# A decoder layer on one core: the input projection in K groups of 2, 2, 4, 4, 4 in place of 4, 4, 4, 4

## The chip, the core and the metric

The kernel runs on one core of a Trainium2 chip. The metric is the device time of one execution in microseconds, lower is better. The core has TensorE (matmuls, weights loaded beside them), VectorE, ScalarE and GpSimd, and SyncE, whose queue here issues every DMA, in order. All are named in the profile as PE (weight loads PEld), DVE, ACT, POOL and SP. Each engine works through its instructions in a fixed order.

## What is computed

One layer over 256 tokens of width 2048, in float32: four token mixers on one shared input projection, an output projection, and a gated feed-forward part, each behind an RMSNorm whose result is scaled and shifted by six modulations that come from a conditioning vector c.

```python
cond = silu(c)
mod = (cond @ w_mod + b_mod).reshape(B, 6, D)          # w_mod: 2048 x 12288
sh1, sc1, g1, sh2, sc2, g2 = [mod[:, i, None, :] for i in range(6)]
h = rmsnorm(x, norm_mix) * (1.0 + sc1) + sh1
proj = h @ w_in                                        # w_in: 2048 x 5660
y = mixers(proj)                                       # GLA, gated DeltaNet, pooling, forgetting attention
x = x + g1 * (y @ w_out)
h = rmsnorm(x, norm_ffn) * (1.0 + sc2) + sh2
x = x + g2 * conv_ffn(h, ...)
out = rmsnorm(x, norm_final)
```

What matters here: no column of the projection can be finished before all 2048 rows of `h` are known, and a row of `h` is known only when its two modulations are summed over all 2048 rows of `w_mod`. A K tile is 128 of those rows of `h`, so there are 16.

## The kernel before

**Precision.** Every weight is loaded as float32 and split into a rounded high part (ScalarE, line 115) and a low part (VectorE, line 100, called from `split`). A product is three matmuls: high by high, high by low, low by high. A load is always [128, 1024] words, 512 KB: four K tiles of 256 columns, or two of 512 (`load_split`, lines 153 to 163; five buffers for loads, three for the parts).

**The groups.** The K tiles are worked through in groups, `GROUPS` (line 46), before 4, 4, 4, 4. For a group three things are needed:

- `mods(g)` (335 to 365) loads w_mod, one DMA for each of the 16 row tiles and always for the columns of this group's shift and scale, 512 KB for four K tiles, and accumulates each on VectorE into one tile `ga` (line 361, the operation at 103 or 107). When the sixteenth is in, TensorE sums `ga` over its partitions (line 345, two instructions for each of 2 x 4 matmuls), VectorE adds the biases (346 to 349), and `h` of the group's K tiles is formed and split into `HL` (`bigA` in the profile). There are five buffers for the loads, `wm`, and one `ga`.
- `gdn(g)` (410 to 424) multiplies the group's K tiles with the 1536 columns of DeltaNet's queries, keys and values. Its sums stay in six PSUM banks (`acc`) over all groups.
- `extras(g)` (470 to 474) visits pairs of column tiles among the other 4096 columns, 16 pairs in all (the comment at line 48 speaks of 18). A visit (`pair`, 438 to 459) loads 256 columns of all K tiles that this pair has not yet had, multiplies them into one of two PSUM banks (`ext`), and adds the bank to the pair's place in SBUF: the first visit by a copy on ScalarE (line 430), the later ones by an addition on VectorE (435, 437, the operation at 100 or 103).

`TAKE` (line 49) says how many of the 16 pairs each group but the last visits, counted from the last pair: 16, 12, 11. In the last group all pairs are visited, with whatever K tiles they still lack; that is 25 loads of 512 KB. These visits are not made beside `gdn` but among the mixers, as filler for TensorE: `gated_deltanet()` is issued first, and the loop at 921 interleaves the visits with the mixers. With each load of a visit, `paced` (908) also takes 0.38 and 0.69 of a step of two background series, the products of c with w_mod for the second half's modulations and the first gate, `bg` (506); what is left of them follows after the mixers.

**The order.** The main loop (lines 510 to 527) interleaves `mods(g + 1)` with `gdn(g)` and `extras(g)`, one w_mod load for each load of weights:

```python
for g in range(NG):
    nxt = mods(g + 1) if g < NG - 1 else iter(())
    with tc.issue_after(hold[0].ins):
        if g == NG - 1:
            small()
            gates()
        for i, _ in enumerate(gdn(g)):
            next(nxt, None)
            if g == 0 and i == 2:
                rest()
                small_load()
```

`issue_after` holds the group's weight loads behind the last w_mod load of the group's own modulations. Within these bounds a scheduler orders each engine's instructions when the kernel is built, by a model of the times; on the chip that order is fixed.

`rest()` (367 to 393) loads thirteen small vectors and constant arrays that the convolution, the mixers and the second half use, and prepares masks from them. `small_load()` (396 to 400) loads 28 narrow columns of w_in with three DMAs of short rows; `small()` (402) multiplies them in the last group, and `gates()` (257) follows.

Of the kernel before, what the change touches and what calls it, by code (L numbers as in the profile page):

```python
# [19 lines left out]
T = 256  # L20
# [8 lines left out]
# columns of w_in  # L29
# [3 lines left out]
# columns of the constant array  # L33
# [11 lines left out]
# the groups of K tiles in which w_in is worked through: first tile, how many  # L45
GROUPS = ((0, 4), (4, 4), (8, 4), (12, 4))
NG = len(GROUPS)
# how many of the 18 pairs of columns beside DeltaNet's queries, keys and values each group but the last visits
TAKE = (16, 12, 11)
# the order of the mixers: gla, pooling, forgetting attention, DeltaNet  # L50
ORDER = "gpfd"
# modulations (s: scale 2, h: shift 2, g: gate 1; half) summed on the tensor engine and on VectorE, steps per load of columns
# [4 lines left out]
def _consts():  # L57
    i = np.arange(P)
    s, t = i[:, None], i[None, :]
    same = (s // CH) == (t // CH)  # L60
    cols = [s == t, same & (s <= t), same & (s > t), s <= t, np.ones((P, P)), s > t]
    cols.append(np.where(t > s, -1e30, 0.0))
    for w in (2, 4, 8, 16):
        cols.append(np.broadcast_to(1.0 / np.minimum(np.arange(1, 17), w), (P, 16)))
    # the level at which s and t part, counted from 1 above the diagonal and from 7 below it
    lv = sum((l + 1) * ((s // (2 * m) == t // (2 * m)) & (s % (2 * m) < m) & (t % (2 * m) >= m))
             for l, m in enumerate(LEVELS))
    lw = lv.T
    cols.append(lv + np.where(lw > 0, lw + len(LEVELS), 0))
    return np.ascontiguousarray(np.concatenate([np.asarray(a, np.float32) for a in cols], axis=1))  # L70
# [3 lines left out]
def trunk_kernel(ctx: ExitStack, tc: tile.TileContext, x, c, w_mod, b_mod, norm_mix, norm_ffn, w_in,  # L74
# [53 lines left out]
    # ones in the rows 0 and 64, and in the rows 32 and 96  # L128
# [45 lines left out]
    def gemv(col0, done, pst=None, ready=lambda: True, bias=None):  # L174
        """cond * w over 1024 columns: without pst summed by partition on VectorE, else on the tensor engine,
        four column tiles side by side"""
        acc = pst() if pst else keep.tile([P, 1024], F32, name="ga", tag="ga")
        if bias is not None:
            G.memset(acc, 0.0)
            nc.sync.dma_start(acc[0:1], bias)  # L180
        for k in range(0, KT, 2):
            wms = []
            for kk in range(2):
                wms.append(wp.tile([P, 1024], F32, name="wm", tag="wm", bufs=4))
                last_wm[0] = nc.sync.dma_start(wms[kk], wm_v[:, k + kk, col0:col0 + 1024])
            for kk in range(2):
                wm = wms[kk]
                if not pst:
                    accumulate(acc, wm, k + kk, bias is None)
                    continue  # L190
                for c in range(2):
                    o = 64 * kk + 32 * c
                    mm(acc[o:o + 32], cond[:, k + kk:k + kk + 1].to_broadcast([P, 32]), wm[:, c * 512:c * 512 + 512],
                       start=k == 0, stop=k == KT - 2)
            if k == KT - 2:
                while not ready():
                    yield
                with tc.high_priority():
                    if pst:
                        gr = wp.tile([P, 1024], F32, name="wr", tag="wr", bufs=5)[:, 0:512]  # L200
                        S_.copy(gr, acc)
                        done([(gr, sel[:, c:c + 1]) for c in range(2)])
                    else:
                        done([(acc[:, c * 512:c * 512 + 512], ones) for c in range(2)])
            yield
# [21 lines left out]
    # ================= attention half =================  # L227
    with ExitStack() as ph:
# [11 lines left out]
        # projections: gla q 0:2, k 2:4, g 4:8, gdn g 8:12, pool 12:16, fox q 16:20, k 20:24  # L240
# [16 lines left out]
        def gates():  # L257
# [13 lines left out]
            # columns 0:4 1/(1+e), columns 4:12 1/(2+e)  # L271
# [16 lines left out]
        with ExitStack() as st:  # L288
# [25 lines left out]
            # 1 + b_mod of the two scales  # L314
# [19 lines left out]
            # sh1, sc1 of the K tiles of group g, then h  # L334
# [60 lines left out]
            # the small columns: lr 0:16, b 16:20, a 20:24, f 24:28; row 28 is one  # L395
# [30 lines left out]
            # one pair of column tiles over some groups of K tiles; two sums share a bank: only the first clears it  # L426
# [68 lines left out]
            # g1 takes the place of values no longer needed  # L495
# [14 lines left out]
# [3 lines that stand above are left out]
# [3 lines left out]
                    for i, _ in enumerate(gdn(g)):  # L516
                        next(nxt, None)
                        if g == 0 and i == 2:
                            rest()
                            small_load()  # L520
# [8 lines left out]
            # conv of gdn's q, k, v straight from the accumulators  # L529
# [37 lines left out]
        def gated_deltanet():  # L567
            # norms of q and k
# [12 lines left out]
            # decays within the chunk  # L581
# [17 lines left out]
            for t in range(NT):  # L599
                ts = slice(t * P, t * P + P)  # L600
                # exp of the decays, transposed: [j, i], i no earlier than j
# [8 lines left out]
                # -M^T (and its diagonal, which no level takes)  # L610
# [9 lines left out]
            # inverse of I + M by blocks of 2, 4, .. 64: X = inverse, Y = its transpose  # L620
# [30 lines left out]
            for t in range(NT):  # L651
                ts = slice(t * P, t * P + P)
                # keys and values by token
# [9 lines left out]
                # attention [j, i]  # L663
# [5 lines left out]
                # queries times the decay from the chunk's start  # L669
# [6 lines left out]
            # u and w^T, over the values' and the keys' place  # L676
# [10 lines left out]
            # the states, chunk by chunk, over M and X  # L687
# [19 lines left out]
            # outputs, normalised, in place of Y  # L707
            oss, ors = dt_("oss", zz), dt_("ors", zz)
            for t in range(NT):
# [12 lines left out]
                # r = c * (c^2 * ss / d + eps)^-1/2  # L722
# [9 lines left out]
        def finish(on_t, t, nw, i, b):  # L732
            """the gate's place takes the gated output, [features, tokens]"""
# [6 lines left out]
        def gla(lp):  # L740
# [4 lines left out]
            # log decays by token, then their sums within the chunk by feature  # L745
# [14 lines left out]
            # attention within the chunk, [s, t], heads by parity: the diagonal, then level by level  # L760
# [29 lines left out]
            # to and from the states  # L790
# [197 lines left out]
    # ================= feed-forward half =================  # L988
    with ExitStack() as ph:
# [3 lines left out]
        with tc.tile_pool(name="hp", bufs=2, reuse_waits="tile") as hp:  # L993
# [7 lines left out]
            # transposed and scaled by the norm in one product  # L1001
# [12 lines left out]
        def proj(gp, view, c0):  # L1014
            """four column tiles, weights stationary: [features, tokens], the high and the low part's sums side by side"""
# [29 lines left out]
        # down: tokens stationary; g2 and the final norm's weight by row  # L1045
# [72 lines left out]
```

## Time and profile before

| what | us |
|---|---|
| median of 3 timed runs | 1316.04 (1313.96 to 1318.38) |
| span of the profiled execution | 1312.4 |
| first accumulation of w_mod on VectorE | 10.76 |
| first matmul of the projection | 40.91 |
| first matmul of the narrow columns (`small`) | 216.44 |
| from 240 to 520 us: TensorE busy | 278.97 of 280 |
| first product of the feed-forward half's transposes | 544.37 |

The profile is one execution, recorded instruction by instruction. A page gives totals; its views give the instructions in order of time (start, duration, engine, line, what is written from what, how many, and in brackets the idle time before and what ended it), groups of like instructions (count, total and mean duration, idle time before), and stretches of time (busy time of each engine, TensorE's granted clock as a share of full speed, share of the DMA engines in use, GB/s). Lines are those of the code; matmuls, VectorE additions and the like all go through small helpers, so they carry the helper's line (97, 100, 103, 107, 112, 115), and the tile's name tells them apart. `acc` is DeltaNet's sums, `ext` the two banks of the pairs (and of small products), `ga` the accumulator of the modulations, `wr`, `wh` and `wl` a load and its two parts.

### The profile page before, as it was taken

What the parts mean: (1) busy time and instruction counts of PE and PEld (TensorE: products, weight loads), DVE (VectorE), ACT (ScalarE), POOL (GpSimd) and SP (SyncE); (2) the same over time, 40 slices, a digit from 0 to 9 for tenths busy, and PEclk for the clock granted to TensorE, in tenths of its full rate; (3) what the DMA queues carried; (4) which work ended last, traced back from release to release, by engine and by line L of the source; (5) the groups of instructions that cost most, each with busy time, mean ns of one, the idle gap of its engine ahead of it and who ended that gap; (6) DMA issues with size and microseconds to landing.
All of it is one profiled execution on the core that took longest, in us unless ns stands there. A gap on an engine that the chain in (4) does not pass through costs nothing.

```text
span 1312.4 us, 20435 instructions
## 1 busy us (share of the span) xinstructions
PE 1257.7 (96%) x7955; PEld 1100.5 (84%) x7955; DVE 886.8 (68%) x1185; ACT 640.7 (49%) x1008; POOL 23.1 (2%) x31
## 2 busy tenths in 40 slices
PE   2799999999999999899999999999999999999996
PEld 1799999898876788888888888888888888888896
DVE  7688797989763497456656665665666587974553
ACT  3455344674364444465545455554555454443432
POOL 0200000010000100000000000000000000000000
PEclk8799999999999999899999999999999999999998
DMA  9999998796567996345565565555655699875552
GB/s 332 287 368 376 312 353 279 259 334 211 176 233 247 328 338 230 125 161 186 170 206 180 189 190 183 190 184 187 191 184 172 206 356 378 304 260 188 192 182 81
DMA packets 174232, 311.95 MB, mean 238 GB/s; under 512 B 16172, under 2 KB 65331, under 8 KB 173495
## 3 DMA queue, kind: packets, MB, share of 16 engines
q1 hardware_dynamic: 174135, 310.65, 70.3%
q8 instruction: 62, 1.02, 0.3%
q14 instruction: 35, 0.29, 0.1%
HBM read 308.51 MB, written 2.10 MB: 237 GB/s over the span
## 4 chain that ended last, share of the span: by engine, by line
PE 91%; DMA 4%; DVE 1%; SPq 1%; ACT 1%; issue 1%; POOLq 0%; POOL 0%; ACTq 0%; DVEq 0%
PE fpt L97 57%; PE ext L97 15%; PE wot L97 5%; PE acc L97 4%; PE gdt L97 4%; PE bgt L97 3%; DMA wm<-in_w_mod_dram 3%; PE oxt L97 2%; DMA wr<-in_w_in_dram 1%; DMA wr<-in_w_out_dram 1%; DVE ga L103 1%; DVE wl L100 0%; ACT h L112 0%; SPq L155 0%; SPq L399 0%
## 5 line engine op out<-in xcount | busy, mean ns | idle before, releaser
L100 DVE TENSOR_TENSOR wl<-wr,wh 128x1024 fp32r<-128x1024 f32 x384 | 468.5, 1223 | 299.7 <-ACT wh L115 298.8
L115 ACT CAST wh<-wr 128x1024 fp32r<-128x1024 f32 x384 | 402.4, 1051 | 497.5 <-PE fpt L97 315.5
L97 PE MATMUL fpt<-bigA,wh 128*128 128x512 f32 x1408 | 485.0, 397 | 0.7 <-ACT h L112 0.7
L97 PE MATMUL fpt<-bigA,wl 128*128 128x256 f32 x1408 | 375.2, 281 | 0.0
L97 PEld LDWEIGHTS fpt<-bigA,wh 128*128 128x128 f32 x1408 | 260.9, 188 | 60.7 <-ACT h L112 0.9
L97 PEld LDWEIGHTS fpt<-bigA,wl 128*128 128x128 f32 x1408 | 259.5, 188 | 5.0
L103 DVE SCALAR_TENSOR_TENSOR ga<-wm,cond,ga 128x1024 f32<-128x1024 f32 x139 | 177.9, 1280 | 9.9 <-DMA wm<-in_w_mod_dram 8.7
L97 PE MATMUL fpt<-wl,AH 128*128 128x512 f32 (+1 forms) x440 | 152.9, 348 | 0.0
L97 PE MATMUL fpt<-wh,AL 128*128 128x512 f32 (+1 forms) x440 | 152.5, 347 | 0.0
L97 PE MATMUL fpt<-wh,AH 128*128 128x512 f32 (+1 forms) x440 | 142.6, 348 | 0.0
L97 PE MATMUL ext<-bigA,wh 128*128 128x256 f32 x768 | 137.9, 281 | 0.0
L97 PEld LDWEIGHTS ext<-bigA,wh 128*128 128x128 f32 x768 | 117.8, 189 | 3.1 <-DVE dS L100 0.8
L97 PE MATMUL ext<-bigA,wl 128*128 128x256 f32 x384 | 107.6, 281 | 1.7 <-DVE wl L100 1.7
L97 PEld LDWEIGHTS fpt<-wh,AH 128*128 128x128 f32 x440 | 83.3, 189 | 10.9 <-ACT wh L115 0.2
L97 PEld LDWEIGHTS fpt<-wh,AL 128*128 128x128 f32 x440 | 83.3, 189 | 10.5 <-issue 0.2
L97 PEld LDWEIGHTS fpt<-wl,AH 128*128 128x128 f32 x440 | 83.3, 189 | 10.5 <-issue 0.2
L97 PEld LDWEIGHTS ext<-bigA,wl 128*128 128x128 f32 x384 | 72.1, 188 | 3.0 <-DVE wl L100 2.1
L97 PE MATMUL acc<-bigA,wh 128*128 128x256 f32 x384 | 69.8, 288 | 4.6 <-ACT bigA L115 2.8
L97 PE MATMUL ext<-wh,bigA 128*128 128x256 f32 (+1 forms) x320 | 68.3, 305 | 0.0
L97 PEld LDWEIGHTS acc<-bigA,wh 128*128 128x128 f32 x384 | 60.1, 196 | 4.9 <-ACT bigA L115 2.9
L97 PE MATMUL wot<-wh,bigA 128*128 128x512 f32 (+1 forms) x256 | 63.0, 337 | 0.0
L97 PEld LDWEIGHTS ext<-wh,bigA 128*128 128x128 f32 x320 | 51.8, 188 | 5.5 <-ACT wh L115 1.7
(335 smaller groups left out, 1193.3 us busy)
## 6 DMA issues: line engine op xcount, KB each, us to landing
wm<-in_w_mod_dram SPq DMA_DIRECT2D x192, 512.0 KB, 6.0
wr<-in_w_in_dram SPq DMA_DIRECT2D x88, 512.0 KB, 9.6
wr<-in_ffn_w_gate_dram SPq DMA_DIRECT2D x88, 512.0 KB, 4.3
wr<-in_ffn_w_up_dram SPq DMA_DIRECT2D x88, 512.0 KB, 3.5
wr<-in_ffn_w_down_dram SPq DMA_DIRECT2D x88, 512.0 KB, 4.5
wr<-in_w_out_dram SPq DMA_DIRECT2D x32, 512.0 KB, 4.1
xt<-in_x_dram SPq DMA_DIRECT2D x2, 1024.0 KB, 7.0
bigC<-in_x_dram SPq DMA_DIRECT2D x2, 1024.0 KB, 11.3
```

The source lines that it names most:

```text
L97: PE.matmul(o, lhsT=l, rhs=r, start=start, stop=stop, skip_group_check=True)
L100: V.tensor_tensor(out=o, in0=a, in1=b, op=op)
L103: V.scalar_tensor_tensor(out=o, in0=a, scalar=s, in1=b, op0=op0, op1=op1)
L115: S_.copy(hi, src)
```

## The change

- The groups are 2, 2, 4, 4, 4 K tiles, so there are five. `mods` of the first two loads half as many columns (16 DMAs of 256 KB each), `gdn` takes 3 loads for each of them instead of 6, and a visit of a pair loads two K tiles, 256 KB, into half of a load buffer.
- `TAKE` becomes 16, 16, 14, 12. The pairs are visited 16 + 16 + 14 + 12 times before the last group, where before it was 16 + 12 + 11; the last group has 22 loads left where it had 25.
- `rest()` is called in the third group (the first K tiles are 4 to 7), and `small_load()` in the fourth (8 to 11), both after the third load of `gdn`, where before both stood in the first group.

Nothing else of what is computed or issued is different. The rest of the diff blanks comments; from line 520 on the changed file's line numbers are one higher.

```diff
-GROUPS = ((0, 4), (4, 4), (8, 4), (12, 4))
+GROUPS = ((0, 2), (2, 2), (4, 4), (8, 4), (12, 4))
 NG = len(GROUPS)
...
-TAKE = (16, 12, 11)
+TAKE = (16, 16, 14, 12)
...
                     for i, _ in enumerate(gdn(g)):
                         next(nxt, None)
-                        if g == 0 and i == 2:
+                        if g == 2 and i == 2:
                             rest()
+                        if g == 3 and i == 2:
                             small_load()
                     if g == NG - 1:
                         break
```

## The prediction

> **What bounds the kernel now.** I read the page's totals first, then the table by stretches, then the engines' rows in order of time up to 245 us, where all lines of the diff act.
>
> ```profile
> span 1312.4 us, 20435 instructions
> ...
> PE 1257.7 (96%) x7955; PEld 1100.5 (84%) x7955; DVE 886.8 (68%) x1185; ACT 640.7 (49%) x1008; POOL 23.1 (2%) x31
> ```
>
> TensorE is busy for 96% of the span, so the share says little. What counts is where it is not busy, or busy at a lower clock.
>
> ```profile
> 0.00:10.00 10.00, 0.33 (x2) 0.28 (x2) 3.83 (x15) 5.81 (x7) 0.20 (x4) 1.00 0.75 277
> 10.00:20.00 10.00, 5.09 (x21) 3.79 (x21) 8.71 (x11) 3.67 (x7) 0.70 (x1) 1.00 1.01 365
> ...
> 40.00:50.00 10.00, 9.09 (x62) 8.77 (x63) 4.78 (x7) 4.63 (x12) 6.41 (x11) 0.77 0.67 105
> 50.00:60.00 10.00, 7.49 (x49) 7.11 (x48) 5.71 (x6) 3.98 (x6) 0.54 (x2) 0.83 1.02 354
> ...
> 75.00:113.00 38.00, 37.99 (x329) 37.80 (x330) 32.57 (x34) 22.86 (x33) 0.00 (x0) 1.00 1.07 372
> 113.00:167.00 54.00, 52.31 (x451) 52.12 (x451) 43.47 (x46) 21.83 (x25) 0.00 (x0) 1.00 0.99 337
> 167.00:213.30 46.30, 46.30 (x397) 46.30 (x396) 42.87 (x45) 18.93 (x20) 0.00 (x0) 1.00 0.98 335
> 240.00:520.00 280.00, 278.97 (x1907) 224.67 (x1905) 202.01 (x322) 143.97 (x296) 11.46 (x8) 1.00 0.76 264
> ```
>
> The columns are the stretch, its length, busy time of PE, PEld, DVE, ACT and POOL, granted clock, DMA share, GB/s. From 75 us on TensorE is the bound. From 240 to 520 it idles for 1 us of 280. Before 75 us it is not: there is a start with hardly a matmul, a stretch at clock 0.77 with the transfers down to 105 GB/s, and one with 7.49 of 10 us busy at 0.83. VectorE and the transfers are close behind, though: 42.87 of 46.30 us (93%) and 0.98 to 1.07.
>
> The start, in order of time:
>
> ```profile
> 4.21 23.90 SPq L360 DMA_DIRECT2D wm<-in_w_mod_dram  x16
> ...
> 10.76 0.75 DVE L107 TENSOR_SCALAR ga<-wm,cond 128x1024 f32<-128x1024 f32 x1 [5.61 <-DMA wm<-in_w_mod_dram]
> ...
> 13.37 2.48 DVE L107 TENSOR_SCALAR xt<-xt,ssm 128x2048 f32<-128x2048 f32 x2
> ...
> 15.76 18.65 DVE L103 SCALAR_TENSOR_TENSOR ga<-wm,cond,ga 128x1024 f32<-128x1024 f32 x14
> ...
> 34.55 3.54 PE L97 MATMUL ext<-ones,ga 128*128 128x1 f32 x16 [12.13 <-DVE ga L103]
> ...
> 40.91 1.65 PE L97 MATMUL acc<-bigA,wh 128*128 128x256 f32 x6 [2.81 <-ACT bigA L115]
> ```
>
> TensorE's first projection matmul (40.91) waits for a chain: 16 loads of w_mod, 16 accumulations on VectorE up to 34.41, 16 small matmuls that sum over partitions, four small steps, the split of h. The change halves the first group, and with it this chain.
>
> **The start.** What an operation of half the width costs follows from the same operation at two widths, and from starts in an unbroken run of VectorE:
>
> ```profile
> L100 DVE TENSOR_TENSOR wl<-wr,wh 128x1024 fp32r<-128x1024 f32 x65 | 79.2, 1220 | 15.6 <-ACT wh L115 15.1
> ...
> L100 DVE TENSOR_TENSOR bigA<-h,bigA 128x256 fp32r<-128x256 f32 x16 | 6.5, 428 | 1.8 <-ACT bigA L115 1.7
> ```
>
> ```profile
> 132.67 1.21 DVE L100 TENSOR_TENSOR wl<-wr,wh 128x1024 fp32r<-128x1024 f32 x1
> 133.80 1.28 DVE L103 SCALAR_TENSOR_TENSOR ga<-wm,cond,ga 128x1024 f32<-128x1024 f32 x1
> 135.00 2.35 DVE L100 TENSOR_TENSOR wl<-wr,wh 128x1024 fp32r<-128x1024 f32 x2
> 137.27 0.68 DVE L100 TENSOR_TENSOR pr<-ext,pr 128x512 f32<-128x512 f32 x1
> 137.87 1.21 DVE L100 TENSOR_TENSOR wl<-wr,wh 128x1024 fp32r<-128x1024 f32 x1
> ...
> 139.00 1.28 DVE L103 SCALAR_TENSOR_TENSOR ga<-wm,cond,ga 128x1024 f32<-128x1024 f32 x1
> ...
> 161.67 0.22 DVE L100 TENSOR_TENSOR md<-ext,V 128x4 f32<-128x4 f32 x2
> ```
>
> 768 columns are worth 1.220 - 0.428 = 0.79 us, so 512 are worth 0.53. By starts a weight split takes 1.13 us (132.67 to 133.80), an accumulation 1.20, a sum from PSUM 0.60; at half width I take 0.60 and 0.67 for the first two.
>
> In the start, 15 accumulations lose 0.53 each (8.0 us), the first product about 0.3, and the first load lands about 0.7 sooner (half of 512 KB at 365 GB/s): 9.0 us, so the accumulations end at 25.4. The transfers keep up: 16 loads of 256 KB are 4.2 MB, 11.5 us at 365 GB/s. The partition sums halve as well, from 3.54 to some 1.8. First projection matmul: 40.91 - 9.0 - 1.8 = 30.1.
>
> **What TensorE then has to do.** No matmul of the projection is added or lost; they change places.
>
> ```profile
> 112.99 16.32 PE acc L97 x144
> ...
> 166.85 16.96 PE acc L97 x144
> 183.81 37.41 PE ext L97 x320
> ```
>
> ```profile
> 211.83 1.84 PE L97 MATMUL ext<-ones,ga 128*128 128x1 f32 x16
> ...
> 216.44 0.40 PE L97 MATMUL ext<-bigA,wsh 128*28 128x256 f32 x2
> ```
>
> One matmul is 16.32/144 = 0.1133 us, a visit of four K tiles to one column pair 24 of them, 2.72 us. There are 16 pairs beside DeltaNet's six. Before, the three groups ahead of the last are (6+16)+(6+12)+(6+11) = 57 units of 24, 155.0 us, plus three partition sums of 1.84 us (5.5). They run from 40.91 to 216.4, 175.5 us: 15 us are lost. Afterwards groups 0 and 1 are 11 units each (29.9 us), group 2 is 20 (54.4), group 3 is 18 (48.9): 60 units. Three units (8.2 us) thus leave the last stage, where TensorE has no idle time (240 to 520, above), and the same 8.2 us are added earlier: neutral in all. The gain is therefore the start plus whatever changes in those 15 us.
>
> **Where the new groups wait.** Group 0: from 30.1, 29.9 us of matmuls, the cold clock's 2.3 us (0.23 of 10 us at 40 to 50), a partition sum of 0.9: 63.2. Group 1 adds 29.9 and 1.8: 94.9. Group 2 needs the modulations of four full tiles by then, and VectorE is what bounds those. Its work, by starts, for group 0: 3 splits of 1.13, 16 of 0.60, 16 half accumulations of 0.67, 1.2 for two tiles of h: 24.9 us. For group 1: 3.4 and 9.6 for splits, 16 sums at 0.60 (9.6; these visits are no longer first ones, so they go from ScalarE's copy to a VectorE add), 16 accumulations of 1.20 (19.2), 2.0 for h: 43.8. Together 68.7 us. VectorE reached 93% in the stretch from 167 and 86% (32.57 of 38) in the one from 75; I take 93%, since it will be the engine waited for: 73.9 us, to 99.3. From the first partition sum to the first matmul took 40.91 - 34.55 = 6.4, less 1.8 at full clock: 4.6. Group 2 starts at 103.9, so TensorE waits 9.0 us and then runs cold again (0.17 of 10 us, as at 50 to 60): 1.7. At 100% it would be 98.7, at 86% 109.9.
>
> ScalarE rounds each half load and, in group 0, copies each pair out:
>
> ```profile
> L115 ACT CAST wh<-wr 128x1024 fp32r<-128x1024 f32 x65 | 68.4, 1052 | 88.8 <-DMA wr<-in_w_in_dram 43.0 <-PE ext L97 26.3 <-PE acc L97 14.7
> ...
> L430 ACT COPY pr<-ext 128x512 f32<-128x512 f32 x9 | 5.3, 587 | 7.1 <-PE ext L97 6.9
> ```
>
> Some 0.6 (a little over half of 1.05) and 0.59 us are 1.2 us per pair, inside the pair's 12 matmuls (1.36): hidden, but with little room.
>
> The transfers are behind VectorE. The loads, by size:
>
> ```profile
> wm<-in_w_mod_dram SPq DMA_DIRECT2D x192, 512.0 KB, 6.0
> wr<-in_w_in_dram SPq DMA_DIRECT2D x88, 512.0 KB, 9.6
> ```
>
> Through group 1 the kernel needs x (2.1 MB), half, half and a whole group of w_mod (4.2, 4.2, 8.4) and four K tiles of w_in (22 loads, 11.5): 30.4 MB. 2.8 MB are in by 10 us (277 GB/s); the rest at 372 GB/s takes 74 us, to 84.
>
> From 103.9: 1.7 + 54.4 + 48.9, two partition sums (3.7), and 1.7 of small stalls as in 113 to 167: the last group starts at 214.3, against 216.4. VectorE's work for group 2 (20 splits, 14 sums, 16 accumulations, h: 52.2) and 3 (18 and 12: 48.7) fits into 56 and 52 us at 93%, to 207. Sum: 2.1 earlier, with 8.2 us less left: **10.3 us**.
>
> **What is moved, and costs nothing by my count.**
>
> ```profile
> 43.25 2.02 SPq L398 DMA_DIRECT2D wsm<-in_w_in_dram  x1
> 45.31 2.31 SPq L399 DMA_DIRECT2D wsm<-in_w_in_dram  x1
> 47.66 1.09 SPq L155 DMA_DIRECT2D wr<-in_w_in_dram  x1
> ```
>
> The thirteen small vectors and three narrow-column loads now stand in the queue while the first group starves: no weight load is issued until 47.66, hence the 105 GB/s. That hole is part of the 15 us lost and leaves the early part. At their new places (group 2 and group 3) five weight buffers of 2.72 us each, 13.6 us, cover their issue; if that cover is gone, the 4.3 us of the two rows above are the price. Their consumers (the convolution, the small product, the gates) come after 214. The last stage has 22 loads instead of 25, and the background sums of shift and gates are paced by these (0.69 steps each), so two steps of two accumulations, 5.1 us, move behind it:
>
> ```profile
> 503.11 1.28 DVE L103 SCALAR_TENSOR_TENSOR ga<-wm,cond,ga 128x1024 f32<-128x1024 f32 x1
> ...
> 517.27 0.69 DVE L100 TENSOR_TENSOR m__5342<-wot,fv 128x512 f32<-128x512 f32 x1 [0.62 <-PE wot L97]
> ```
>
> The last of them ends at 504.4 and the gate is first used at 517.3: 13 us of cover. Once it is gone, each further us is paid.
>
> **Against the median.** The profiled span is 1312.4, the median of the timed runs 1316.0, 3.6 more; I take the difference off the median: 1316.0 - 10.3 = 1305.7, and from 1300.5 (VectorE at 100%) to 1311.7 (at 86%).
>
> **Rivals.**
> - *No wait ahead of group 2.* Accumulations ran ahead in the profile: the third set's last started at 139.00, 22 us before it was used (161.67). If that holds here, group 2 starts at 94.9 with no cold restart, the last group at 203.6: 12.8 + 8.2 = 21 us, 1295. Against it: 68.7 us of VectorE beside 61 of TensorE leave no room. Chance 0.13.
> - *The sum over partitions comes late.* The same rows speak for this: TensorE reads the accumulator in its fixed order, 22 us after it was complete, and there is only one accumulator, so the next set starts after that. If the second set, complete near 52, is read only when group 0 ends (63.2), everything behind moves 11 us: 1316.7, no change. Chance 0.17.
> - *Half-size loads come at half the rate.* Then the start takes as long as before but for the 1.8 us: 1314.7. Against it, the 512 KB loads ran back to back at 365 GB/s with five in flight. Chance 0.06. The Trainium skill (DMA: Bandwidth & Descriptors, Bandwidth) asks for transfers of 1 MiB and more, and has 341 GB/s at 1 MB and 138 at 64 KB; the trace's 365 at half a megabyte already lies above that, and no run here shows a quarter.
> - *TensorE does not get its clock: slower.* A pair in groups 0 and 1 is 12 matmuls, 1.36 us, while VectorE needs 0.60 + 0.60 + 1.20 = 2.4 us for it in group 1, and both sum banks wait for it. Such broken work was granted 0.83 at 50 to 60, with 49 matmuls where 88 fit. At clock c the two groups take 59.8/c us; at 0.83 VectorE still hides that, at 0.65 group 2 starts at 30.1 + 2.7 + 92.0 = 124.8, 20.9 us late: 1326.6. It makes the kernel slower than before by over 4 us from about 0.70 down. Against it: 0.83 in the only such stretch. Chance 0.14. The Trainium skill (TensorE: Matmul & The Clock Gate, Part 1) says half rate is the default and only some 3.4 us of sustained work lift it, which would hold this rival's clock near half and give some 1354, an estimate; the row at 50 to 60 contradicts that for a half-filled stretch.
>
> **How the numbers follow.** Forecast 0.50, rivals 0.13, 0.17, 0.06, 0.14. A measurement can tell about 0.3%, 4 us. Faster by more: 0.50 + 0.13 = 0.63. Within: 0.17 + 0.06, of which 0.01 I give to slower: 0.22. Slower: 0.15. The range runs from 1296, leaving out half of the first rival, to 1322, leaving out most of the last: 0.18 outside.
>
> **What would show it.** The changed profile should show accumulations of 128x512 ending near 25, the first projection matmul near 30, weight loads with no gap at 40 to 50, a TensorE wait of 5 to 15 us ended by VectorE's accumulation near 95 to 110, and the last group's first matmul near 214. A first matmul later than 35, a granted clock under 0.7 from 30 to 100, or a last group later than 222 would prove me wrong.

## The result and the profile after

The changed kernel takes 1327.06 us (median of 4 runs, 1325.87 to 1329.24), the kernel before, on the same chip, 1315.48. The ratio is 1.0089, with a 95% interval of 1.0073 to 1.0105: slower by 0.9%, where 1305.7 was forecast. Medians and ratios in this document leave out three executions that took far longer than the others of their kernel: 2533.8 us (the profiled one of e2, whose steps are therefore not given), 1791.5 (one of e4) and 3719.0 (one of the kernel before).

The page's totals after:

```profile
span 1326.0 us, 20645 instructions
...
PE 1267.7 (96%) x7955; PEld 1105.6 (83%) x7955; DVE 900.7 (68%) x1239; ACT 643.0 (48%) x1024; POOL 24.2 (2%) x31
```

TensorE has the same 7955 instructions and the same 96%. VectorE has 54 more. The table by stretches, in the same columns as before:

```profile
10.00:20.00 10.00, 5.27 (x21) 3.90 (x21) 8.68 (x14) 3.81 (x7) 1.28 (x1) 1.00 0.74 231
...
40.00:50.00 10.00, 9.60 (x82) 9.24 (x81) 9.11 (x14) 5.20 (x9) 0.00 (x0) 1.00 0.88 272
50.00:60.00 10.00, 8.68 (x73) 8.26 (x72) 4.34 (x7) 5.61 (x10) 0.00 (x0) 1.00 1.04 357
75.00:113.00 38.00, 29.45 (x228) 28.08 (x227) 34.20 (x43) 11.40 (x19) 8.28 (x12) 0.95 0.92 303
113.00:167.00 54.00, 53.45 (x431) 53.01 (x431) 47.95 (x53) 22.95 (x30) 0.00 (x0) 0.94 1.02 331
167.00:213.30 46.30, 45.27 (x372) 45.02 (x372) 43.69 (x48) 19.32 (x24) 0.00 (x0) 0.96 1.04 363
240.00:520.00 280.00, 278.24 (x1928) 223.97 (x1927) 204.71 (x346) 147.00 (x305) 11.15 (x10) 0.99 0.78 264
```

Read the counts in brackets, not the busy time: from 75 to 113 us TensorE did 329 matmuls before and 228 now. The hole at 40 to 50 us is gone (82 for 62), but from 75 on the stretches that were full are no longer so. The counts show what busy time hides: at a granted clock of 0.50 TensorE is busy for all of 2 us with 11 matmuls, at 1.00 with 20 (rows at 110 and 120 us, below).

**The start.** VectorE and then TensorE, in order of time:

```profile
10.30 0.49 DVE L107 TENSOR_SCALAR ga<-wm,cond 128x512 f32<-128x512 f32 x1 [5.15 <-DMA wm<-in_w_mod_dram]
...
13.27 2.48 DVE L107 TENSOR_SCALAR xt<-xt,ssm 128x2048 f32<-128x2048 f32 x2 [0.59 <-POOL ssm L320]
15.66 5.47 DVE L103 SCALAR_TENSOR_TENSOR ga<-wm,cond,ga 128x512 f32<-128x512 f32 x7
...
23.99 3.11 DVE L103 SCALAR_TENSOR_TENSOR ga<-wm,cond,ga 128x512 f32<-128x512 f32 x4 [0.67 <-DMA wm<-in_w_mod_dram]
```

```profile
27.25 1.84 PE L97 MATMUL ext<-ones,ga 128*128 128x1 f32 x8 [5.13 <-DVE ga L103]
33.33 1.55 PE L97 MATMUL acc<-bigA,wh 128*128 128x256 f32 x5 [4.25 <-ACT bigA L115]
```

The accumulations end at 27.1 (25.4 was forecast) and the first projection matmul starts at 33.3 (30.1). Seven accumulations in one unbroken row from 15.66 mean that loads had landed and were waiting: five of them held every buffer while VectorE normalised x (13.27 to 15.75), and no further load could be issued. The transfers from 10 to 34 us, in slices of 0.6 us (busy share in tenths, then GB/s):

```profile
DMA  9999999910004889998799989988989999999999
GB/s 355 350 341 353 341 292 319 338 56 0 0 0 126 283 251 254 297 353 239 210 287 328 314 256 288 309 321 268 297 323 374 338 384 393 391 386 376 355 352 352
```

From 14.8 to 15.4 us they fall to 56 GB/s, and to 17.2 they stand still. So the 231 GB/s of this stretch comes from a pause of about 2 us: five buffers hold half as many microseconds of transfers when each holds half as much.

**The second set of modulations.** VectorE, then the sum over partitions:

```profile
49.56 1.53 DVE L103 SCALAR_TENSOR_TENSOR ga<-wm,cond,ga 128x512 f32<-128x512 f32 x2
51.01 1.28 DVE L100 TENSOR_TENSOR wl<-wr,wh 128x512 fp32r<-128x512 f32 x2
53.98 0.69 DVE L100 TENSOR_TENSOR wl<-wr,wh 128x512 fp32r<-128x512 f32 x1 [1.68 <-ACT wh L115]
...
67.70 0.23 DVE L100 TENSOR_TENSOR md<-ext,V 128x2 f32<-128x2 f32 x2 [1.24 <-PE ext L97]
67.85 0.74 DVE L107 TENSOR_SCALAR ga<-wm,cond 128x1024 f32<-128x1024 f32 x1
```

```profile
66.72 0.95 PE L97 MATMUL ext<-ones,ga 128*128 128x1 f32 x8
```

The set is complete at 51.1. TensorE sums it at 66.7, after 3 steps of DeltaNet and 13 of the 16 pairs, with no idle time ahead of it: that is its place in TensorE's fixed order. There is one accumulator, so the third set's first product can't start before 67.85. VectorE, the engine that the forecast took to be full (93%) from 25.4 us on, is busy 4.34 of 10 us here (50 to 60, above), and 6.66 of the 16.61 us from 51.09 to 67.70.

**The third set.** From 67.70 on VectorE is all but full: 40.18 of 41.93 us to the end of the last accumulation (109.63). One period of three us, and the end:

```profile
90.56 0.68 DVE L100 TENSOR_TENSOR wl<-wr,wh 128x512 fp32r<-128x512 f32 x1
91.15 0.68 DVE L100 TENSOR_TENSOR pr<-ext,pr 128x512 f32<-128x512 f32 x1
91.75 1.27 DVE L103 SCALAR_TENSOR_TENSOR ga<-wm,cond,ga 128x1024 f32<-128x1024 f32 x1
92.95 0.68 DVE L100 TENSOR_TENSOR wl<-wr,wh 128x512 fp32r<-128x512 f32 x1
...
108.32 1.31 DVE L103 SCALAR_TENSOR_TENSOR ga<-wm,cond,ga 128x1024 f32<-128x1024 f32 x1
113.36 0.23 DVE L100 TENSOR_TENSOR md<-ext,V 128x4 f32<-128x4 f32 x2 [2.45 <-PE ext L97]
```

The last accumulation ends at 109.6 us; 99.3 was forecast for that. The set is read at 113.4, because TensorE's sum of it takes 3.55 us, as long as a sum at half clock took at the start of the kernel before (1.84 at full clock). TensorE had waited, and the clock was gone:

```profile
109.78 3.55 PE L97 MATMUL ext<-ones,ga 128*128 128x1 f32 x16 [4.04 <-DVE ga L103]
...
110.00:112.00 2.00, 2.00 (x11) 2.00 (x11) 0.91 (x2) 0.00 (x0) 1.75 (x5) 0.50 0.92 261
...
118.00:120.00 2.00, 2.00 (x15) 2.00 (x14) 2.00 (x5) 1.52 (x2) 0.00 (x0) 0.69 1.06 390
120.00:122.00 2.00, 2.00 (x20) 2.00 (x18) 2.00 (x3) 1.71 (x4) 0.00 (x0) 1.00 1.05 384
```

**The narrow columns**, now in the fourth group, on SyncE's queue:

```profile
141.96 0.94 SPq L397 DMA_DIRECT2D wsm<-in_w_in_dram  x1
142.95 7.13 SPq L398 DMA_DIRECT2D wsm<-in_w_in_dram  x1
150.12 1.12 SPq L399 DMA_DIRECT2D wsm<-in_w_in_dram  x1
151.34 1.64 SPq L155 DMA_DIRECT2D wr<-in_w_in_dram  x1
```

The issue of one load of short rows took 7.13 us (2.02 before), and for 9.4 us (141.96 to 151.34) no load of weights or of w_mod was issued. The last stage begins at 235.3 us (216.4 before, 214.3 forecast).

### The profile page after: what moved, and what is told of

Read it like the earlier page. It is cut to its first block, busy times and chain, and to the rows that moved or that the text cites. A ratio compares the mean times of both kernels' runs of the same rounds, so it can differ in the third digit from the quotient of the medians.

```text
span 1326.0 us, 20645 instructions
## 1 busy us (share of the span) xinstructions
PE 1267.7 (96%) x7955; PEld 1105.6 (83%) x7955; DVE 900.7 (68%) x1239; ACT 643.0 (48%) x1024; POOL 24.2 (2%) x31
## 4 chain that ended last, share of the span: by engine, by line
PE 88%; DMA 5%; DVE 3%; ACT 2%; issue 1%; SPq 0%; POOL 0%; POOLq 0%; ACTq 0%; DVEq 0%
PE fpt L97 56%; PE ext L97 11%; PE acc L97 5%; PE wot L97 5%; PE gdt L97 4%; DMA wr<-in_w_in_dram 3%; PE bgt L97 3%; PE oxt L97 2%; DMA wm<-in_w_mod_dram 2%; DVE ga L103 1%; DVE wl L100 1%; ACT wh L115 1%; ACT h L112 0%; DVE pr L100 0%; DVE bigA L100 0%
## 5 line engine op out<-in xcount | busy, mean ns | idle before, releaser
L100 DVE TENSOR_TENSOR wl<-wr,wh 128x1024 fp32r<-128x1024 f32 (+1 forms) x400 | 470.9, 1180 | 302.3 <-ACT wh L115 301.6
L115 ACT CAST wh<-wr 128x1024 fp32r<-128x1024 f32 (+1 forms) x400 | 405.2, 1016 | 503.9 <-PE fpt L97 315.7
L103 DVE SCALAR_TENSOR_TENSOR ga<-wm,cond,ga 128x1024 f32<-128x1024 f32 (+1 forms) x154 | 181.0, 1175 | 13.2 <-DMA wm<-in_w_mod_dram 12.3
L97 PE MATMUL acc<-bigA,wh 128*128 128x256 f32 x384 | 69.4, 286 | 4.8 <-ACT bigA L115 4.2
L97 PE MATMUL ext<-wh,bigA 128*128 128x256 f32 (+1 forms) x320 | 71.8, 314 | 1.4 <-DVE pr L100 1.0
```

Of the source, the lines that this page charges most:

```text
L97: PE.matmul(o, lhsT=l, rhs=r, start=start, stop=stop, skip_group_check=True)
L100: V.tensor_tensor(out=o, in0=a, in1=b, op=op)
L103: V.scalar_tensor_tensor(out=o, in0=a, scalar=s, in1=b, op0=op0, op1=op1)
L115: S_.copy(hi, src)
```

## The experiments

Times of the steps are from the trace of each run. The runs were on several chips, so compare them by the ratio to the kernel before on the same chip. "2nd" and "3rd" are when VectorE reads the summed modulations of that set (in four-group kernels the 2nd set is that of K tiles 4 to 7), "last" is the first matmul of the narrow columns, "stage" the time from there to the feed-forward half.

| kernel | 2nd | 3rd | last | stage | median | ratio (95%) |
|---|---|---|---|---|---|---|
| before | 96.2 | 161.7 | 216.4 | 327.9 | 1315.5 | 1 |
| after | 67.7 | 113.4 | 235.3 | 322.6 | 1327.1 | 1.0089 (1.0073 to 1.0105) |
| e1 small loads early | 71.1 | 113.8 | 228.1 | 323.0 | 1319.6 | 1.0032 (1.0018 to 1.0047) |
| e2 small loads late, four groups | | | | | 1318.0 | 1.0024 (1.0014 to 1.0034) |
| e3 two accumulators | 69.4 | 123.4 | 248.3 | 324.5 | 1341.8 | 1.0204 (1.0180 to 1.0229) |
| e4 w_mod sooner | 54.2 | 115.4 | 232.5 | 323.0 | 1325.4 | 1.0086 (1.0061 to 1.0111) |
| e5 w_mod sooner, small loads early | 65.0 | 117.2 | 232.3 | 324.0 | 1325.4 | 1.0072 (1.0057 to 1.0087) |
| e6 narrow columns late | 70.2 | 112.9 | 232.8 | 323.2 | 1325.2 | 1.0066 (1.0051 to 1.0082) |
| e7 groups 2, 4, 4, 4, 2 | 79.9 | 135.2 | 239.0 | 341.1 | 1349.9 | 1.0253 (1.0235 to 1.0271) |
| e8 fewer visits | 70.7 | 113.4 | 221.6 | 335.0 | 1326.4 | 1.0080 (1.0063 to 1.0097) |
| e9 no second additions | 71.0 | 112.9 | 231.0 | 320.2 | 1321.7 | 1.0043 (1.0026 to 1.0060) |
| e10 more visits, four groups | 97.0 | 162.6 | 225.2 | 321.6 | 1318.0 | 1.0013 (1.0002 to 1.0024) |
| e11 eight buffers | 75.4 | 117.5 | 232.4 | 323.2 | 1325.9 | 1.0068 (1.0053 to 1.0083) |
| e12 all three limits | 54.0 | 93.2 | 236.5 | 323.5 | 1329.4 | 1.0098 (1.0072 to 1.0124) |
| e13 two of three | 55.7 | 95.2 | 234.3 | 323.4 | 1328.7 | 1.0092 (1.0068 to 1.0116) |
| e14 additions left out, small loads late | 68.8 | 104.8 | 233.5 | 321.7 | 1325.1 | 1.0077 (1.0051 to 1.0103) |
| e15 16, 10, 12, 11 visits | 54.4 | 94.7 | 219.5 | 351.3 | 1340.9 | 1.0186 (1.0163 to 1.0208) |
| e16 small loads last, four groups | 88.9 | 153.4 | 215.3 | 329.2 | 1315.6 | 0.9996 (0.9986 to 1.0006) |
| e17 small loads last, five groups | 68.3 | 110.9 | 239.2 | 333.7 | 1340.1 | 1.0185 (1.0157 to 1.0213) |

**The small loads: e1, e2, e6.** e1 is the changed kernel with both calls back in the first group; e2 the kernel before with `rest()` in its second and `small_load()` in its third group; e6 the changed kernel with `rest()` back in the first group and `small_load()` still in the fourth.

```diff
-                        if g == 2 and i == 2:
+                        if g == 0 and i == 2:
                             rest()
-                        if g == 3 and i == 2:
                             small_load()
```

> The five groups and the new visits, with the thirteen small vectors and the narrow columns back in the first group. Theory A (the second set of modulations is read late: its partition sum stands behind 13 of 16 pairs in TensorE's order, and the one accumulator keeps the third set waiting, 51 to 68 us): the wait stays, so at least 1325. Theory B (the moved loads hold up the weight loads at their new places, 93 to 109 and 142 to 154 us): about 8 us come back, 1319. Theory C (VectorE is simply full in the second group, with half-size operations): no change, 1327.

> The old four groups and old visits, the small vectors moved to the group of K tiles 4 to 7 and the narrow columns to that of 8 to 11: the placement alone. Theory A and C: the hole at 40 to 50 us goes and nothing takes its place, 5 us faster than before, 1310. Theory B: the hole only moves, and is paid at the new places, 1315 to 1320.

> The changed kernel with the thirteen vectors back in the first group and only the narrow columns late, in the group of K tiles 8 to 11. If the narrow columns (short rows, 142 to 154 us in the queue) are what costs: the fourth set is read near 172 and the time is 1325 or more. If the thirteen vectors are: 1320, as with both early. Shared: 1322.

The last stage begins at 228.1 in e1, 7.2 us earlier than after, and the median falls by 7.5 us. The third set is read at the same time, so all of it lies behind: 114.3 us from that read to the last stage for 121.9. Of the 0.57 points of the ratio the narrow columns alone take 0.34 (e6 against e1; each ratio is known to about 0.15). In four groups the late place costs 0.24%. The early hole was therefore no loss that disappears when the loads leave it; what it costs where is taken up with e16 and e17. What remains, 0.32%, belongs to the groups and the visits.

**The late sum over partitions: e3, e4, e5.** e3 gives the odd sets an accumulator of their own. e4 takes two loads of w_mod for each load of weights in group 0, so that the second set's sum stands behind 5 pairs instead of 13; e5 is the same on e1.

```diff
                     for i, _ in enumerate(gdn(g)):
                         next(nxt, None)
+                        if g == 0:
+                            next(nxt, None)
...
                     for _ in extras(g):
                         next(nxt, None)
+                        if g == 0:
+                            next(nxt, None)
```

> The changed kernel with a second accumulator for every other set of modulations. Theory A: the third set starts near 52 instead of 68 and ends near 97 instead of 110; 8 to 12 us faster than the change, 1315 to 1319. Theory B: no change, 1327. Theory C: VectorE has the same work in the second group and the earlier start only fills its idle time of 50 to 67; under 4 us.

> The changed kernel, taking two loads of w_mod with each load of weights in the first group, so that the partition sum stands behind 5 of 16 pairs instead of 13. Theory A: as with two accumulators, the third set starts near 52, 1315 to 1319. Theory B: 1327. Theory C: under 4 us.

> New groups and visits, the small loads back in the first group (1319.6 in the run before), and two loads of w_mod with each load of weights in the first group, so that the second set is read 13 us sooner. Theory A (late read, hidden in the earlier run of this edit because the moved vectors then fell on the wait): third set read near 103 instead of 114, 1309 to 1312. Theory C (VectorE and the transfers are full up to the third set, whatever the order): the third set is still read near 112, 1317 to 1320.

In e4 the second set is read at 54.2, 13.5 us sooner, and nothing is gained: VectorE completes the third set at 88.8 instead of 109.6, but it is read at 115.4, and the time is as after. e5 is slower than e1. e3 shows the same more plainly; VectorE, then a stretch:

```profile
83.34 3.92 DVE L103 SCALAR_TENSOR_TENSOR ga<-wm,cond,ga 128x1024 f32<-128x1024 f32 x3
...
123.37 0.22 DVE L100 TENSOR_TENSOR md<-ext,V 128x4 f32<-128x4 f32 x2
```

```profile
40.00:120.00 80.00, 65.65 (x477) 61.93 (x476) 69.56 (x88) 34.37 (x58) 8.17 (x12) 0.91 0.99 341
```

With two accumulators the third set is complete at 87.3, 36 us before it is read. TensorE reaches the read late: it does 477 matmuls in these 80 us, 512 after. What it waited for most from 60 to 124 us were weights not yet rounded by ScalarE (6.4 us in all), which come from the loads. Loads of w_mod that come sooner are issued ahead of weights, and the transfers (0.99) have nothing to spare.

**VectorE's additions: e9.** On e1, the sixteen additions of the second group's visits are left out.

```diff
-                    add(dst, a, g0 == 0, scale)
+                    if g0 != 1:
+                        add(dst, a, g0 == 0, scale)
```

> New groups and visits, small loads early (1319.6), and the sixteen additions of the second group's visits left out, so that the sums of K tiles 2 and 3 are missing from those columns: 9.6 us less for VectorE. Theory C (VectorE, with the halved operations and the second group's additions, is what holds the third set): third set read at 104 to 107 instead of 114, and 6 to 10 us faster, 1310 to 1314. Theory A or transfers as the bound: under 3 us.

```profile
101.63 1.28 DVE L103 SCALAR_TENSOR_TENSOR ga<-wm,cond,ga 128x1024 f32<-128x1024 f32 x1
...
112.92 0.23 DVE L100 TENSOR_TENSOR md<-ext,V 128x4 f32<-128x4 f32 x2 [0.76 <-PE ext L97]
```

VectorE is now done with the third set at 102.9 (106.5 in e1), and the set is read 10 us later, at 112.9 (113.8 in e1). In e1 itself the set was complete 7.3 us before it was read, so VectorE was not what held it there. Taking away any one limit uncovers the next.

**The start: e11.** On e1, three more buffers for half-size loads.

> New groups and visits, small loads early, and eight buffers instead of five for the half-size loads of w_mod. If five loads of 256 KB in flight are what kept the transfers at 231 to 250 GB/s from 10 to 20 us: 350 GB/s there, the first projection matmul 2 to 3 us sooner, at 30; the total gains 0 to 3 us. If the half-size loads themselves are slow: no change of that rate.

The transfers at 10 to 20 us rise from 231 to 312 GB/s, so the pause was one of buffers. VectorE has done 14 of the 16 accumulations at 24.2. But the first projection matmul moves from 32.7 to 38.9, although the first load of weights is issued sooner (19.95 for 22.49), because the engines' fixed orders came out differently: the last two accumulations stand behind the split of a weight (27.43) and end at 30.1, and transposes of the small vectors stand ahead of the first matmul on TensorE, where they wait for their loads until 37.7. So the gain from the deeper queue was not seen by itself.

**The visits: e10, e8, e15, and e7.** e10 is the kernel before with 16, 14, 12 visits; e8 is e1 with 16, 16, 12, 11, so that the work left for the last stage is that of the kernel before. e7 is e1 with groups of 2, 4, 4, 4, 2 and 16, 12, 11, 11 visits.

> The old four groups and the old place of the small loads; only the second and third group visit 14 and 12 pairs instead of 12 and 11, which leaves 22 loads for the last stage as in the change. If the three visits are neutral, as predicted: 1314 to 1317. If their 8.2 us come back only in part (5 us in the changed profile's last stage): 1317 to 1319. If, as between the runs with new and old visits, the last stage gains more: 1308 to 1311.

> New groups, small loads early, but 12 and 11 visits in the third and fourth group as before, so the last stage keeps 25 loads: what the three visits made earlier are worth. If they are neutral, as predicted: 1319 to 1320. If the last stage keeps only 5 of the 8.2 us, as its length in the changed profile says: 1316 to 1317.

> Groups of 2, 4, 4, 4, 2 with 16, 12, 11, 11 visits, small loads early: the short first group stays, but the second group has four tiles, so VectorE's accumulations fall on twice the matmuls. Theory C: the start's 7 us stay and TensorE no longer waits in the second group: the third set's place (K tiles 6 to 9) is reached by 120 and the time is 1307 to 1311. Theory A: the read of the second set stays late, and the time is 1315 or more.

e10: the last stage begins 8.8 us later and is 6.3 us shorter; measured 0.13%. In four groups that step of the forecast was nearly neutral, as it said. e8: its last stage begins 5.2 us after that of the kernel before, for the same work in total, although its first matmul comes 8.2 us earlier (32.8 for 40.9). So the five groups give back some 13 us. Its time, 1326.4, is above what either reading expected: against e1 the three visits left for the last stage make that begin 6.5 us sooner and last 12.0 longer. It takes 335.0 us where the kernel before takes 327.9, with 2280 matmuls in both: 5.6 us of the difference are busy time (328.7 for 323.1), 1.4 idle time. In e7 it lasts 341.1. So its length does not follow from the number of visits alone. What sets it was not settled.

**All at once: e12 to e15.** e12 has the small loads in the fourth group, two w_mod steps in groups 0 and 1, and no second additions; e13 is e12 with the additions; e14 is e12 with one w_mod step; e15 is e13 with 16, 10, 12, 11 visits.

> The changed kernel with three limits of the third group's modulations eased at once: the thirteen vectors and the narrow columns both load in the fourth group, groups 0 and 1 take two loads of w_mod for each load of weights instead of one, and the additions of the second group's visits into SBUF are left out, so that the projection lacks K tiles 2 and 3 in its pairs. If three limits stand close behind one another (TensorE's late read of the accumulator, VectorE's work, the transfers), the third set is read by about 104 us instead of 113.4 and the last stage begins near 225 instead of 235.3 but for what the narrow columns cost. If the transfers alone bound it, it is still read at 110 or later and nothing is gained.

> As the kernel with all three limits eased, but with the additions of the second group's visits kept, so only the late read and the vectors' place in the queue are eased. If VectorE is the next limit, the third set is read some 5 to 8 us later than there (16 additions of about 0.6 us), at about 110. If the transfers alone bound it, both are read at the same time, within 2 us.

> As the kernel with all three limits eased, but with one load of w_mod for each load of weights as in the changed kernel; the additions of the second group's visits are left out here too. If TensorE's place for the read is a limit of its own, the accumulations of the third set end near 102 and it is still read at 110 to 113. If only the transfers and VectorE count, it is read within 3 us of the end of its accumulations.

> As the kernel with two limits eased, and the pairs visited 16, 10, 12, 11 times before the last group instead of 16, 16, 14, 12: with fewer half-size visits in the second group VectorE has six splits and six additions less there (7 us) and the transfers 1.5 MB. If these bound the third set, it is read near 104, and the last stage begins earlier by about 8 us plus the work that it then has to do itself (its 11 visits of two to four K tiles more), so that the time comes near that of the kernel before, 1316. If the new groups cost by their broken work instead, the time stays at 1321 or above.

The third set is read at 93 to 105 in all four, as the theory of three limits had it. But in e12, e13 and e14, which have the visits of the changed kernel, the last stage begins at 236.5, 234.3 and 233.5, within 2 us of after (235.3), which that theory had wrong: a third set read up to 20 us sooner was not a last stage reached sooner. e12 by stretches, then e14:

```profile
40.00:120.00 80.00, 73.41 (x569) 69.83 (x568) 70.50 (x89) 38.66 (x66) 0.00 (x0) 0.96 1.04 362
120.00:180.00 60.00, 52.87 (x410) 51.51 (x409) 36.38 (x41) 23.09 (x27) 7.07 (x12) 0.91 0.87 259
```

```profile
40.00:120.00 80.00, 74.50 (x608) 72.43 (x607) 65.12 (x85) 41.19 (x68) 0.00 (x0) 0.98 0.98 335
```

In e12 the transfers are full up to 120 (1.04), and TensorE does 569 matmuls where 80 us hold 706 (at 0.1133 us): with the order eased the transfers are the limit. Then the small loads come, and 410 are done where 530 fit, 13.6 us lost. In e13 the additions changed the third set's read by only 2 us, not the 5 to 8 of VectorE as the limit. In e14, with the transfers freed and the additions gone, the set ends at 102.7 and is read at 104.8: TensorE's place for it held only as long as TensorE was starved. e15 is slower still: the lighter second group didn't help, and with 28 units of visits left for it (25 before) the last stage took 351.3 us.

**The small loads where the transfers have room: e16, e17.** Both calls behind the last w_mod load of all, in four groups and in five.

```diff
...
                 hold[0] = last_wm[0]
+                if g == NG - 2:
+                    with tc.issue_after(hold[0].ins):
+                        rest()
+                        small_load()
```

> The kernel before, with the thirteen vectors and the three loads of narrow columns queued behind the last load of w_mod of the last group, in place of the first group. If the hole that they make costs about 7 us of TensorE at 40 to 60 us (111 matmuls there, where two stretches of 10 us hold 176) and nothing behind the last w_mod load, where the transfers have room (322 and 254 GB/s at 200 to 220), the last stage begins near 210 instead of 216.4 and the time is some 1309, a ratio near 0.995. If the hole is paid wherever it stands, the ratio is 0.999 to 1.004. If the small product then waits for its columns, the last stage begins later than 218 and it is slower.

> The changed kernel with the thirteen vectors and the narrow columns queued behind the last load of w_mod of the last group. If the small loads were 7 us of its loss (as the kernel with both early says) and cost nothing there, the time is near 1319 or below and the last stage begins near 226; if they cost in the first group and in this place alike, it stays at 1320 to 1324. If the five groups as such are slower, it does not come below 1316 in any case; at 1310 or below the groups would gain and the small loads alone would have lost it.

The kernel before, e16, and e17, by stretches:

```profile
40.00:120.00 80.00, 74.98 (x611) 73.88 (x612) 62.06 (x61) 42.03 (x63) 6.94 (x12) 0.95 1.01 336
40.00:60.00 20.00, 16.58 (x109) 15.88 (x110) 10.49 (x13) 8.61 (x18) 6.94 (x12) 0.80 0.84 229
...
200.00:220.00 20.00, 20.00 (x174) 19.65 (x173) 15.93 (x21) 9.69 (x14) 0.00 (x0) 1.00 0.87 288
```

```profile
40.00:120.00 80.00, 78.83 (x666) 78.83 (x667) 68.38 (x66) 42.12 (x59) 0.00 (x0) 0.97 1.07 373
40.00:60.00 20.00, 18.83 (x152) 18.83 (x153) 17.05 (x18) 8.42 (x13) 0.00 (x0) 0.89 1.06 375
...
200.00:220.00 20.00, 15.44 (x104) 13.93 (x103) 12.62 (x19) 8.32 (x16) 1.08 (x4) 0.83 1.03 358
```

```profile
40.00:120.00 80.00, 70.17 (x536) 67.47 (x536) 66.15 (x92) 39.07 (x66) 0.00 (x0) 0.94 0.98 327
```

In e16 the early hole is really gone: 152 matmuls for 109 at 40 to 60 us, the third set 8.3 us sooner. It is then paid at 200 to 220, 104 for 174: 70 x 0.1133 = 7.9 us. The time is the same. So in four groups the small loads cost some 8 us of TensorE at either place. In five groups the place matters. e17 has no small load before 191 us and reads its fourth set at 164.4; e1, with the loads early, reads it at 166.3, 1.9 us later, and after, with the loads in the third and fourth group, at 172.3, 7.9 later. e17 pays behind that: 74.8 us from there to the last stage, for 61.8 in e1. So the early place was the cheapest of the three, in one trace of each.

The two kernels also show the groups by themselves, with no small load before 175 us. In the 80 us from 40 on, four groups do 666 matmuls and lose 4.5 us; five do 536 and lose 19.3. That is 14.8 us, against a first matmul 8.2 us earlier (33.0 for 41.2). Against e14, whose 608 differ in that stretch by the additions left out, 72 matmuls or 8.2 us of the loss are the sixteen additions. That does not hold in every setting: e9 did 520 in that stretch, e1 with the additions 528.

In e17 the last stage begins still later than after (239.2) and lasts 11 us longer; TensorE idles for 13.1 us of it, 5.6 after, and why is open. No version here beats the kernel before.

## Why the prediction was wrong

Against its own sum the last stage began 21.0 us late and saved 2.9 us less, 23.9 us in all: 1302.1, the forecast of the span, became 1326.0. The parts:

- **The start, 3.2 us of these.** 33.3 for 30.1. "The transfers keep up" failed: VectorE's 2.48 us on x stopped them with all buffers full, and the accumulations ended 1.7 us late. The other 1.5 us lie between partition sum and first matmul. The rival of half-size loads at half rate is refuted all the same: 256 KB loads ran at 341 to 355 GB/s from 10 to 13 us, ahead of the pause. The Trainium skill (DMA: Bandwidth & Descriptors, Bandwidth) asks for 1 MiB and more, and has 341 GB/s at that size for loads issued from GpSimd; these loads, a quarter of that and issued from SyncE, reached as much.
- **The third set: the step that failed.** "VectorE is what bounds those", at 93% from 25.4 to 99.3, and with it the path from there to the last stage. VectorE's work was sized well: 65.3 us were done where 68.7 were reckoned. But it was busy for only 79% of the time from 27.1 to 109.6, because it could not run through: "the sum over partitions comes late" held, the second set being complete at 51.1 (52 in the rival) and read by TensorE's sum at 66.7 (63.2). That is 10 us of VectorE idle, and the third set ended 10.3 us late. I had it as a rival at 0.17 with the row in hand. Nor was VectorE the bound when the wait was gone: e4 ended the set at 88.8 and read it at 115.4. And the read did not set the last stage: e13 read the set 18 us sooner and reached the last stage 1.0 us sooner. What the runs show in place of the one bound is three limits close behind one another (place of the sum, VectorE, transfers); e4, e9, e12 and e14 each take away one or more and meet another. A forecast that takes the largest and fills it evenly is below all of them together. With the small loads early (e1) the last stage began at 228.1, so 13.8 of the 21.0 us belong to the five groups, the start among them. How the 14.8 us by which five groups lose more than four from 40 to 120 us divide is not shown; the additions are up to 8.2 of them.
- **What is moved, 7.2 us (e1 to after).** "Costs nothing" failed. In five groups the hole at the early place was worth 1.9 us, and the late places cost 7.9 up to the fourth set alone, above the 4.3 named "if that cover is gone". That the consumers come after 214 held for most; TensorE's transposes of the small vectors begin at 124.1, without a wait. The mistake was the row: the issue time on SyncE's queue is not the price. In the changed kernel the buffers did cover the narrow columns up to 160 us, but weights landed late behind them, and from 160 to 175 TensorE did 102 matmuls where 132 fit, the last 5 us at a granted clock of 0.66.
- **The units** were right: three left the last stage. It became 5.3 us shorter, not 8.2 (6.3 in e10), so in four groups the move costs 2 to 3 us where I had it neutral; between e8 and e1 it gained 5.5.
- **The cold restart** was priced at 1.7 us. From 110 to 120 us 51 matmuls were done where 88 fit: 4.2 us.
- **TensorE's clock**, the rival that gave 1326.6, met the number by chance: from 40 to 100 us the clock was 1.00, with 61 to 82 matmuls per 10 us. Work that filled 70 to 93% of the time kept its clock; it was lost behind a wait of 4.04 us.
- **The signs.** TensorE's wait for VectorE came, but lasted 4.04 us where 5 to 15 was named (it ended at 109.8). Of the three that would prove the forecast wrong, the last group later than 222 came true (235.3); the first matmul came before 35 (33.3), and the clock was under 0.7 from 30 to 40 us alone (0.63).

## What to carry to other kernels

Where several resources are each nearly full, price a change by what each of them allows one after the other, and doubt a gain that rests on one of them running evenly. A hole in a full queue is a price, not an opportunity: moving the loads moves the hole, and only a run in which it has gone from one place and not come up in another shows a saving. Cutting a reduction into smaller groups shortens the start once, but adds an accumulation into SBUF and the fixed part of each smaller operation to every group. Before sizing a limit, take it away in a run and see whether the end moves: here the step that looked like the bottleneck could be had 18 us sooner and the end stayed where it was.

## What the runs showed of the hardware

- After the 4.04 us wait ahead of the third sum, TensorE was busy without a gap and was still granted 0.50 for 8 us (110 to 118, 11 matmuls per 2 us), then 0.69 and 1.00. The Trainium skill (TensorE: Matmul & The Clock Gate, Part 1) has some 3.4 us of sustained work lift half rate. The first 3.5 us here were one-column sums; counted from their end (113.3) the half clock lasted about 6 us, and from the first projection matmul (33.3) about 4 (to 37.4). In the same run a sum of 1.84 us and a wait of 0.97 together (166.5 to 169.3) were followed by 0.61 and 0.54 from 170 to 174, while waits of up to 1.34 us between projection matmuls left the clock at 1.00 (40 to 100). Both would fit sums that do not count as work; that was not tried.
- The issue of one load of short rows (8 columns of 2048 rows) held SyncE's queue for 7.13 us after, for 2.02 in the kernel before, and for 3.54 and 3.80 in e16 and e17. After, the transfers still ran at 364 to 366 GB/s from 142 to 146 us with the loads issued ahead of it; before, they were down to 19 from 42 to 44. That fits an issue that waits for the loads ahead; it was not tried.
- A queue of five loads stops completely (no byte from 15.4 to 17.2 us) when the engine that frees the buffers does 2.48 us of other work and each load takes 0.7 us (256 KB at the 365 GB/s of the kernel before); with 512 KB loads and the same work the stretch from 10 to 20 us held 365 GB/s, and with eight buffers for 256 KB loads 312 (e11).
